# Group A of a hybrid trunk step: both values pieces of a step in one run, the recurrence in front of the fourth transposes

## The chip, the cores and the metric

The kernel runs on one core of one Trainium2 chip. The metric is the device time of the program in microseconds (us), from the start of its execution to its end. Three runs of the kernel before took 3770.87, 3778.68 and 3775.09 us: the median is 3775.09 us.

## The reference

The program is one layer of a trunk with a token mixer and a feed-forward network, for 256 context tokens and 2048 latent tokens of width 1024, all in float32. The token mixer has three groups of heads:

```python
# A: 6 query heads, 2 key/value heads of width 64, latent queries over 2048 latent + 256 context keys
sc = einsum('bqhgd,bkhd->bhgqk', q_blk, k) * scale
p = softmax(sc, axis=-1)
o = einsum('bhgqk,bkhd->bqhgd', p, v)
# B: 4 heads, two directions, chunks of 64 tokens; the recurrence over the chunks:
v_new = u_i - w_i @ s
o_i = (q_i * exp(g_i)) @ s + a_i @ v_new
s = s * exp(g_last) + einsum('bhcd,bhce->bhde', k_i * exp(g_last - g_i), v_new)
# C: 6 heads, neighbourhood attention with a bias, plus the context keys
```

Context queries of group A see the 256 context keys only. The outputs of the groups are joined, projected, normalised and go through the feed-forward network. The change touches the order of the work while group A runs; what is computed stays the same.

## The kernel before, in words

The program runs in stages: projection (`phase_b`, to about 500 us of the profile), preparation, group A (`group_a`, about 820 to 1643 us), group C (`group_c`, to about 1975 us), output projection, feed-forward network. Group B's recurrence (`recur`) has no stage of its own: it is a Python generator, and whoever runs group A or C takes one piece of it at a time with `next(rec, None)`.

**Group A.** There are 18 query tiles of 128 tokens, two to a group: groups 0 to 7 are latent tiles, group 8 the two context tiles. A group has three head pairs (`pr`), a head pair two heads (`h2`), a head two query tiles (`qi`): 12 steps per group. A step of a latent group does the following.

- It makes the scores of one head and one query tile against 2304 keys in three PSUM tiles `Sa` (1024), `Sb` (1024) and `Sc` (256); behind each, VectorE takes the row maxima (L1229) and TensorE runs one piece of the list `trs`.
- VectorE joins the three maxima (L1233), and ScalarE makes the exponentials of the three tiles into `P` (L1237). In the loop over these, pieces of other work are put in by hand, behind the first exponential (`i == 0`) and behind the second (`i == 1`).
- At its end, five transposing pieces of this step's `P` are appended to `trs`; they run during the next step.

A step of the context group has a single score tile (`n = 1`), a single exponential, and so only `i == 0`.

The lists of pieces are these. `trs`: a piece transposes four (the last: two) 128x128 blocks of `P` on TensorE into a PSUM tile `pt`, and ScalarE copies it to `PT` (L1043). `pvs`: the products with the values of the head pair before; eight pieces that each take two or three key blocks (`po`, 8 or 12 matmul instructions), and a ninth, `fin`, that transposes the result (`oT`) and scales it. `late` holds a `fin` that is due: one per head pair, so it comes in the first step of the next head pair but one. `extra` holds, in the first two head pairs of a group, an empty piece and two pieces that transpose the next group's queries (`q_stack`, `qd`). `one(q)` runs the next piece of a list, if there is one; `one(late or extra)` takes from `late` first. By these rules steps 0, 2, 3, 4, 6, 7 and 8 of a group have a late or extra piece that does work.

**The recurrence.** Its first three pieces load and prepare; then three pieces follow for each of 36 chunk pairs `n`: `w @ s` and its subtraction (L972, L983; POOL makes `Se`, L980), `v_new` (L989, L994), and outputs with the new state (L1001 to L1014, then DMAs, L1016). For even `n` the first kind has a merge for the next tile in it (`merge_u`, 32 instructions, L924, L927), and so has the second (`merge_t`, L939, L943). Each piece needs the VectorE work of the piece before. A piece starts by taking a PSUM tile `rx` with `self.rpt()`. The recurrence begins at step `RA = 6` of group A, counted over all groups (`12 * g + 4 * pr + 2 * h2 + qi`), so its loop starts at step 9 and repeats every six steps. What is left of it goes on in group C, one piece per unit from unit 6, where a unit is one head and one query tile.

**What sets the order.** TensorE's instructions are kept in program order (`self.pe` is an `InOrder`, switched on in L2108), so the place of a piece in the source is its place in TensorE's queue. The other engines' orders, DMA issues among them, come from a scheduler that goes by program order, by readiness and by priority (`tc.high_priority` moves the maxima ahead). PSUM tiles come from pools: `Sa`, `Sb` and `Sc` have one buffer each, `po` one, and the pool `A_t` (L1108) has two buffers of 2 KB under the one tag `pt`. All of `trs`, `fin`, `q_stack` and the recurrence (L1110, named `rx`) take their tile from these two; a buffer is free again when all its readers are done.

Nearly all TensorE instructions are recorded under line 37 (the `InOrder` helper), so they are told apart by tile names.

Of the kernel before, what the change touches and what calls it, by code (L numbers as in the profile page):

```python
# [59 lines left out]
class K:  # L60
# [1014 lines left out]
    def q_stack(self, t, h0, h1, pst):  # L1075

        if h0 == 0:
            self.Q[t] = [self.qp[t // 2 % 2].tile([128, 6, 128], F32R, tag=f"q{n}", name="q", bufs=2) for n in "hl"]
        self.q_split(self.Q[t][0][:, h0:h1], self.Q[t][1][:, h0:h1], self.qds[t][:, h0:h1], h1 - h0, pst)

    def q_load(self, t, pool, bufs):
        qd = self.qds[t] = pool.tile([128, 6, 2, 64], F32, tag="qd", name="qd", bufs=bufs)
        for r in range(2):
            self.sp.dma_start(qd[:, :, r, :], self.qa_d[:, t, :].rearrange("p (h d) -> p h d", d=64))
# [13 lines left out]
    def group_a(self):  # L1098
# [3 lines left out]
        with ExitStack() as es:  # L1102
# [7 lines left out]
            rec = self.rec = self.recur(self.rwk, lambda: pst.tile([128, 512], F32, tag="pt", name="rx"))  # L1110
# [46 lines left out]
            def turn(P, PTh, nk, qi):  # L1157

                def piece(k0):
                    m = min(4, nk - k0)  # L1160
                    p = pst.tile([128, 512], F32, tag="pt", name="pt")
                    for j in range(m):
                        self.pe.transpose(p[:, 128 * j:128 * j + 128],
                                          P[:, 128 * (k0 + j):128 * (k0 + j) + 128], self.ident)
                    self.evac(0, PTh[:, k0:k0 + m, 128 * qi:128 * qi + 128],
                              p[:, :128 * m].rearrange("p (j t) -> p j t", j=m))
                return [lambda k0=k0: piece(k0) for k0 in range(0, nk, 4)]

            trs, pvs, late, extra = [], [], [], []

            def one(q):
                if q:
                    q.pop(0)()

            def drain():
                for q in (trs, late, pvs, extra):
                    while q:
                        one(q)

            for g in range(len(groups)):  # L1180
                lat = g < 8
                nk = NT if lat else 2
                ks = KS if lat else KSp
                parts = [(0, 1024, "a"), (1024, 2048, "b"), (2048, 2304, "c")] if lat else [(0, 256, "")]
                n = len(parts)
                if not lat:
                    drain()
                    kc = tp.tile([128, NT, 256], F32, tag="PT", name="kc").rearrange("p a b -> p (a b)")
                    for h in range(2):
                        kv = kc[:, 2048 * h:2048 * h + 1024].rearrange("p (t r d) -> p t r d", t=8, r=2)  # L1190
                        for r in range(2):
                            nc.sync.dma_start(kv[:, :, r, :], self.c_d[1][:, h, 0:8, :])
                        for q in range(2):
                            extra.append(lambda kv=kv, h=h, q=q: self.k_split(
                                KS, kv[:, 4 * q:4 * q + 4], [(h, 4 * q + i) for i in range(4)], pst))
                    kx = kc[:, 4096:4608].rearrange("p (h t r d) -> p h t r d", h=2, t=2, r=2)
                    for h in range(2):
                        for r in range(2):
                            nc.sync.dma_start(kx[:, h, :, r, :],
                                              a["cache_c_k"][0, 0][:, h, :].rearrange("(t p) d -> p t d", p=128))  # L1200
                for pr in range(3):
                    if g + 1 < len(groups):
                        if pr < 2:
                            t = groups[g + 1][pr]
                            q_load(t)
                            extra += [lambda: None, lambda t=t: q_stack(t, 0, 4), lambda t=t: q_stack(t, 4, 6)]
                    PT = [tp.tile([128, NT, 256], F32, tag="PT", name="PT") for _ in range(2)]
                    rs = sp.tile([128, 2, 2], F32, tag="rs", name="rs", bufs=3)
                    for h2 in range(2):
                        h = 2 * pr + h2  # L1210
                        kv = h // 3
                        for qi in range(2):
                            qh, ql = (x[:, h, :] for x in Q[groups[g][qi]])
                            mx = sp.tile([128, 4], F32, tag="mx", name="mx", bufs=4)
                            sm = sp.tile([128, 4], F32, tag="sm", name="sm", bufs=4)
                            P = sp.tile([128, 2304], F32, tag="P", name="P")
                            Ss = []
                            for i, (lo_, hi_, nm) in enumerate(parts):
                                nm = nm or "abc"[(2 * h2 + qi) % 3]
                                S = psS.tile([128, 1024 if nm != "c" else 256], F32, tag="S" + nm, name="S" + nm)  # L1220
                                Ss.append(S)
                                for c0 in range(lo_, hi_, 512):
                                    c1 = min(c0 + 512, hi_)
                                    self.pe.matmul(S[:, c0 - lo_:c1 - lo_], lhsT=qh, rhs=ks[:, kv, c0:c1],
                                                   start=True, stop=False)
                                    self.pe.matmul(S[:, c0 - lo_:c1 - lo_], lhsT=ql, rhs=ks[:, kv, c0:c1],
                                                   start=False, stop=True)
                                with tc.high_priority(offset=1000):
                                    nc.vector.tensor_reduce(mx[:, i:i + 1], S[:, :hi_ - lo_], AX.X, ALU.max)  # L1229
                                one(trs)  # L1230
                            with tc.high_priority(offset=1000):
                                if n > 1:
                                    nc.vector.tensor_reduce(mx[:, 3:4], mx[:, 0:n], AX.X, ALU.max, negate=True)  # L1233
                                else:
                                    nc.vector.tensor_scalar(mx[:, 3:4], mx[:, 0:1], -1.0, None, ALU.mult)
                            for i, (lo_, hi_, nm) in enumerate(parts):
                                nc.scalar.activation(P[:, lo_:hi_], Ss[i][:, :hi_ - lo_], AF.Exp, bias=mx[:, 3:4],  # L1237
                                                     accum_out=sm[:, i:i + 1])
                                if i == 0:
                                    one(pvs)  # L1240
                                    one(trs)
                                    one(late or extra)
                                if i == 1:
                                    one(pvs)
                                    if 12 * g + 4 * pr + 2 * h2 + qi >= self.RA:
                                        next(rec, None)
                                    one(trs)
                            if n > 1:
                                nc.vector.tensor_reduce(sm[:, 3:4], sm[:, 0:n], AX.X, ALU.add)
                            nc.vector.reciprocal(rs[:, qi, h2:h2 + 1], sm[:, 3:4] if n > 1 else sm[:, 0:1])  # L1250
                            self.bg.run(2.0)
                            trs += turn(P, PT[h2], nk, qi)
                    if pvs:
                        late.append(pvs.pop())
                        while pvs:
                            one(pvs)
                    pvs += pv_pieces(g, pr, PT, rs)
# [960 lines left out]
```

## Time and profile before

| what | us |
|---|---|
| median of three runs | 3775.09 |
| the three runs | 3770.87, 3778.68, 3775.09 |
| the profiled execution | 3773.57 |
| its span, from the first to the last instruction | 3771.8 |
| group A, first score tile to last exponential | 819.5 to about 1641 |
| its last 12 steps (context group) | 1618.7 to about 1643 |
| pieces of the recurrence in group C | 1668.4 to about 1755 |

The granted TensorE clock was 0.984 on average over the span and 1.00 in group A from 900 us on. Durations in the timeline are those of instructions, which overlap on TensorE; the distance from the start of one group of matmuls to the start of the next is what a group costs.

### The profile page before, as it was taken

Reading aid. Unit: us, or ns where it says so; the run is one execution under the profiler, and the core shown is the slowest. Engines: PE = TensorE matmul, PEld = TensorE weight load, DVE = VectorE, ACT = ScalarE, POOL = GpSimd, SP = SyncE. Lnnn points to the kernel's source line nnn. Section 1 sums busy time; section 2 is a strip of 40 time slices with the busy share of each in tenths; the row PEclk is TensorE's granted clock in tenths of the full one; section 3 lists DMA queues with packets and bytes.
Section 4 is the critical chain, followed back from the end, with each engine's and each line's share of the span. In section 5 each row is a group of like instructions: output and inputs, shape, how many; then the busy total and the mean of one; then the engine's idle time right before and its main releaser. Section 6 shows DMA issues by size and latency. Waiting matters only on the chain.

```text
span 3771.8 us, 64758 instructions
## 1 busy us (share of the span) xinstructions
PE 3598.5 (95%) x24526; PEld 3154.2 (84%) x24526; DVE 2406.1 (64%) x5044; ACT 1721.0 (46%) x3541; POOL 590.1 (16%) x861
## 2 busy tenths in 40 slices
PE   8997999969999999989999989999999999999999
PEld 6886988966777777768887879999999999888887
DVE  6684477689755555558774667778778777422433
ACT  4223322236666666656775663344334334322321
POOL 0002322630000000000003411111111111000121
PEclk9998999989999999999999999999999999999999
DMA  8556877841121211155314663334334333634553
GB/s 308 183 201 182 258 224 219 206 119 47 43 53 52 53 53 52 49 142 163 99 54 164 218 189 98 102 99 126 99 98 126 102 98 93 194 116 128 199 183 128
DMA packets 647640, 501.67 MB, mean 133 GB/s; under 512 B 253521, under 2 KB 576960, under 8 KB 644768
## 3 DMA queue, kind: packets, MB, share of 16 engines
q1 hardware_dynamic: 644544, 493.93, 43.6%
q8 instruction: 193, 3.16, 0.4%
q10 hardware_dynamic: 2624, 3.55, 0.3%
q14 instruction: 119, 0.97, 0.1%
q0 software_dynamic: 160, 0.05, 0.0%
HBM read 348.66 MB, written 148.73 MB: 132 GB/s over the span
## 4 chain that ended last, share of the span: by engine, by line
PE 73%; DVE 13%; ACT 4%; DMA 4%; POOL 3%; issue 2%; SPq 1%; ACTq 0%; DVEq 0%; POOLq 0%
PE pd L37 15%; PE Y L37 10%; PE pso L37 8%; PE pt L37 7%; PE X L37 7%; PE Z L37 7%; PE po L37 6%; PE rx L37 3%; PE Sa L37 2%; DVE stmp L852 2%; PE S L37 2%; PE Sb L37 2%; DVE mx L1229 2%; PE m L37 2%; DVE sW L853 1%
## 5 line engine op out<-in xcount | busy, mean ns | idle before, releaser
L1043 ACT ACTIVATE PT<-pt 128x512 f32<-128x512 f32 (+1 forms) x600 | 332.3, 554 | 256.8 <-PE pt L37 250.0
L37 PE MATMUL Y<-hop,raw 128*128 128x384 f32 x1788 | 337.3, 337 | 5.0 <-DVE u L1929 2.9
L37 PEld LDWEIGHTS Y<-hop,raw 128*128 128x128 f32 x1788 | 313.9, 187 | 6.7 <-DVE u L1929 3.8
L37 PE MATMUL po<-PT,V 128*64 128x256 f32 (+1 forms) x3072 | 314.7, 342 | 2.2 <-ACT PT L1043 1.9
L37 PE MATMUL pso<-whi,hi 128*128 128x384 f32 (+2 forms) x864 | 288.5, 334 | 26.0 <-ACT whi L261 14.0
L37 PE MATMUL pt<-ident,P 128*128 128x128 f32 x1752 | 285.0, 280 | 15.1 <-ACT PT L1043 7.9
L37 PE MATMUL pso<-whi,lo 128*128 128x384 f32 (+2 forms) x864 | 282.4, 327 | 7.7 <-DMA lo<-hl 7.7
L37 PE MATMUL pso<-wlo,hi 128*128 128x384 f32 (+2 forms) x864 | 282.6, 327 | 0.8 <-DVE wlo L262 0.5
L37 PEld LDWEIGHTS pt<-ident,P 128*128 128x128 f32 x1752 | 200.3, 141 | 94.6 <-ACT PT L1043 35.9
L37 PEld LDWEIGHTS po<-PT,V 128*64 128x64 f32 x3072 | 181.3, 137 | 79.3 <-issue 33.8
L37 PE MATMUL X<-hop,raw 128*128 128x384 f32 x1176 | 223.4, 338 | 4.1 <-DVE raw L1766 2.3
L37 PE MATMUL Z<-hop,raw 128*128 128x384 f32 x1188 | 223.6, 336 | 0.0
L1766 DVE TENSOR_TENSOR raw<-S,raw 128x512 fp32r<-128x512 f32 x198 | 145.2, 734 | 110.7 <-ACT raw L1765 105.7
L37 PEld LDWEIGHTS X<-hop,raw 128*128 128x128 f32 x1176 | 208.0, 188 | 5.1 <-DVE raw L1766 3.1
L37 PEld LDWEIGHTS Z<-hop,raw 128*128 128x128 f32 x1188 | 208.7, 187 | 0.1
L1765 ACT ACTIVATE raw<-S 128x512 fp32r<-128x512 f32 x198 | 124.3, 629 | 172.0 <-PE X L37 66.1
L1947 POOL TENSOR_TENSOR o<-sg,p 128x384 f32<-128x384 f32 x66 | 89.2, 1352 | 711.6 <-DVE p L1946 350.8
L37 PEld LDWEIGHTS pso<-whi,hi 128*128 128x128 f32 x864 | 168.1, 195 | 30.5 <-ACT whi L261 15.6
L37 PE MATMUL pd<-wd,ao 128*128 128x512 f32 x756 | 185.5, 394 | 0.0
L37 PE MATMUL pd<-wd,hop 128*128 128x512 f32 x756 | 183.0, 392 | 0.0
L980 POOL TENSOR_TENSOR rSe<-rS,eh 64x128 f32<-64x128 f32 x144 | 54.9, 400 | 811.8 <-DVE rS L1012 780.9
L37 PEld LDWEIGHTS pso<-whi,lo 128*128 128x128 f32 x864 | 167.6, 194 | 10.9 <-DMA lo<-hl 9.1
(360 smaller groups left out, 8283.9 us busy)
## 6 DMA issues: line engine op xcount, KB each, us to landing
hr<-a SPq DMA_DIRECT2D x72, 704.0 KB, 4.5
wr<-in_w_gu_dram SPq DMA_DIRECT2D x66, 512.0 KB, 4.0
wr<-in_w_gu_dram SPq DMA_DIRECT2D x132, 256.0 KB, 3.1
a<-o SPq DMA_DIRECT2D x396, 64.0 KB, 1.6
wm<-in_w_mod_dram SPq DMA_DIRECT2D x48, 512.0 KB, 4.4
hi<-hh SPq DMA_DIRECT2D x36, 512.0 KB, 5.0
lo<-hl SPq DMA_DIRECT2D x36, 512.0 KB, 6.1
st<-ptk SPq DMA_DIRECT2D x18, 768.0 KB, 3.9
```

Of the source, the lines that this page charges most:

```text
L37: r = f(*x, **kw)
L852: v.tensor_tensor(tv, M[:n, c0:c1, c0:i], M[:n, c0:i, i].unsqueeze(1).to_broadcast([n, m, k]), ALU.mult)
L853: v.tensor_reduce(M[:n, c0:c1, i], tv, AX.X, ALU.add)
L980: nc.gpsimd.tensor_tensor(Se[hh[x], d], S[hh[x], d, :, hh[x]], e.unsqueeze(2).to_broadcast([64, 2, 64]), ALU.mult)
L1043: self.nc.scalar.activation(out, p, AF.Copy)
L1229: nc.vector.tensor_reduce(mx[:, i:i + 1], S[:, :hi_ - lo_], AX.X, ALU.max)
L1765: self.nc.scalar.activation(hi, raw, AF.Copy)
L1766: self.nc.vector.tensor_tensor(lo, raw, hi.bitcast(F32), ALU.subtract)
L1947: nc.gpsimd.tensor_tensor(o[:, 0], sg, p1, ALU.mult)
```

## The change

Two places in the loop over the exponentials change. Behind the first exponential the values piece is taken out, and the recurrence's piece (with its condition) takes its place in front of the fourth transposing piece. Behind the second exponential two values pieces follow one another, and then comes the fifth transposing piece.

```diff
                                 if i == 0:
-                                    one(pvs)
+                                    if 12 * g + 4 * pr + 2 * h2 + qi >= self.RA:
+                                        next(rec, None)
                                     one(trs)
                                     one(late or extra)
                                 if i == 1:
                                     one(pvs)
-                                    if 12 * g + 4 * pr + 2 * h2 + qi >= self.RA:
-                                        next(rec, None)
+                                    one(pvs)
                                     one(trs)
```

A latent step still runs two values pieces, two transposing pieces, one late or extra piece and one piece of the recurrence in this loop. In the context group, where only `i == 0` is reached, a step used to run a values piece and no piece of the recurrence; now it runs a piece of the recurrence and no values piece, and the values pieces run in the loop at the end of the head pair (L1253 to L1256), which is not changed.

## The prediction

> **What bounds the kernel now.** I read the page first, for the span and the engine that fills it.
>
> ```profile
> span 3771.8 us, 64758 instructions
> PE 3598.5 (95%) x24526; PEld 3154.2 (84%) x24526; DVE 2406.1 (64%) x5044; ACT 1721.0 (46%) x3541; POOL 590.1 (16%) x861
> ```
>
> The profiled run took 3773.57 us, 1.8 us more than its span; the median of the three timed runs is 3775.09, so the sum below is made against 3773.6 and 1.5 us are within the spread. A busy share over the whole program says little about one stage, so next came the table by stage: one stretch of group A's even part, and the whole of its last 12 short steps (the context query tiles). Columns: stretch, length, busy time of PE, weight loads, DVE, ACT, POOL, granted clock, DMA.
>
> ```profile
> 1100.00:1200.00 100.00, 98.70 (x968) 75.29 (x964) 55.83 (x121) 68.67 (x143) 6.05 (x16) 1.00 0.19 50
> 1618.70:1643.00 24.30, 17.35 (x104) 10.88 (x103) 13.39 (x50) 14.42 (x45) 0.39 (x3) 1.00 0.06 18
> ```
>
> In the even part TensorE is busy 98.7 of 100 us and the others far less: a microsecond in which TensorE stands still is a microsecond of the end, and no other engine is close. In the last 12 steps TensorE has 24.3 - 17.35 = 7 us free. TensorE issues in program order, so the order of the pieces is the subject. Part of the timeline of one even step with a piece of the recurrence and one "late" piece (here `oT`) follows; columns: start, length, engine, line, what.
>
> ```profile
> 1212.47 0.60 PE L37 MATMUL pt<-ident,P 128*128 128x128 f32 x4
> 1212.82 1.17 PE L37 MATMUL Sb<-KA,q 128*128 128x512 f32 x4
> ...
> 1214.46 1.28 ACT L1043 ACTIVATE PT<-pt 128x512 f32<-128x512 f32 x2 [0.76 <-PE pt L37]
> 1214.51 0.60 PE L37 MATMUL pt<-ident,P 128*128 128x128 f32 x4
> 1215.04 1.08 PE L37 MATMUL po<-PT,V 128*64 128x256 f32 x8
> ...
> 1215.87 1.12 ACT L1237 ACTIVATE P<-Sa,mx 128x1024 f32<-128x1024 f32 x1
> 1216.05 0.66 PE L37 MATMUL pt<-ident,P 128*128 128x128 f32 x4
> 1216.54 0.38 PE L37 MATMUL pt<-ident,oT 128*128 128x128 f32 x2
> 1216.86 1.08 PE L37 MATMUL po<-PT,V 128*64 128x256 f32 x8
> ...
> 1217.45 1.12 ACT L1237 ACTIVATE P<-Sb,mx 128x1024 f32<-128x1024 f32 x1
> 1217.78 0.66 PE L37 MATMUL rx<-rS,rsT 128*64 128x128 f32 x8
> ...
> 1218.36 0.44 PE L37 MATMUL pt<-ident,P 128*128 128x128 f32 x2
> 1218.47 0.87 DVE L983 TENSOR_TENSOR rv<-rst,rx 64x256 f32<-64x256 f32 x2 [1.02 <-PE rx L37]
> ```
>
> Matmuls overlap, so I price by the distance of starts. The order is: third transposing piece (1214.51), a values piece (`po`), fourth transposing piece (1216.05), late piece (1216.54), values, recurrence (`rx`), fifth transposing piece (1218.36). Transposes, late pieces and recurrence all take their PSUM from one pool of two buffers (`pt`, the same pool as `rx`). That is the resource the change touches: whoever holds a buffer long must have other work behind him.
>
> **The change, part by part.** In a step with three score tiles the recurrence piece goes from between the second values piece and the fifth transposes to between the third and the fourth transposes; both values pieces come together after the late piece. No instruction is added or removed.
>
> (a) The late piece behind the recurrence. New order of buffer takers: third transposes, recurrence, fourth transposes, late, fifth. With two buffers the late piece needs the one that the recurrence holds (or the one of the fourth transposes, which ScalarE empties no sooner, behind an exponential). Before, the recurrence piece was followed by transposes 5, a score tile and transposes 1 before its buffer mattered; now only the fourth transposes lie between. Call E the start of TensorE's next work after the recurrence piece. Without a wait the late piece would start at E + 0.49 (1216.54 - 1216.05: the length of four transposes). With it, it starts when VectorE has read the buffer. The recurrence has three kinds of piece, and two of them also carry, every other round, the merge for the next tile:
>
> ```profile
> 1194.15 0.44 PE L37 MATMUL pt<-ident,P 128*128 128x128 f32 x2
> 1194.25 0.29 DVE L927 TENSOR_TENSOR rU<-rx,nb 128x128 f32<-128x128 f32 x1 [3.73 <-PE rx L37]
> 1194.46 0.86 DVE L983 TENSOR_TENSOR rv<-rst,rx 64x256 f32<-64x256 f32 x2
> ```
>
> ```profile
> 1202.11 0.44 PE L37 MATMUL pt<-ident,P 128*128 128x128 f32 x2
> 1202.22 1.19 DVE L943 COPY rsy<-rx 32x128 f32<-32x128 f32 x4 [3.56 <-PE rx L37]
> 1203.42 0.42 DVE L994 COPY rv<-rx 64x256 f32<-64x256 f32 x1
> ...
> 1205.33 0.60 ACT L1043 ACTIVATE PT<-pt 128x512 f32<-128x512 f32 x1 [0.78 <-PE pt L37]
> 1205.98 0.66 PE L37 MATMUL pt<-ident,P 128*128 128x128 f32 x4 [0.45 <-ACT PT L1043]
> ...
> 1209.51 0.66 PE L37 MATMUL rx<-rS,rsT 128*64 128x128 f32 x8
> 1211.26 0.44 PE L37 MATMUL pt<-ident,P 128*128 128x128 f32 x2
> 1211.43 0.87 DVE L1012 TENSOR_TENSOR rS<-rSe,rx 64x256 f32<-64x256 f32 x2 [0.34 <-PE rx L37]
> ...
> 1212.33 0.42 DVE L1014 COPY ro<-rx 128x256 f32<-128x256 f32 x1
> ```
>
> A released buffer is used 0.05 us later (the transfer of 1205.33 ends at 1205.93, the transposes start at 1205.98, after a wait that shows what a held buffer does). So the buffer is free at: first kind without merge, 0.11 + 0.87 + 0.05 = E + 1.03 (E is 1218.36); with merge, 1195.32 - 1194.15 + 0.05 = E + 1.22; second kind without merge, 0.11 + 2 x 0.42 + 0.05 = E + 1.00; with merge, 0.11 + 1.19 + 2 x 0.42 + 0.05 = E + 2.19; third kind, 1212.75 - 1211.26 + 0.05 = E + 1.54. Less 0.49, TensorE waits 0.54, 0.73, 0.51, 1.70 and 1.05 us. VectorE is then free (it has finished the step's maxima and the next tile of scores comes later), so nothing queues ahead of these reads.
>
> How often: a late piece with work comes, by the code, in 7 of 12 steps (one `oT` per head pair; four query pieces in the first eight steps). The recurrence loop starts in step 9, has period 6, so the pairing is fixed: steps 0 and 6 of a group meet the first kind plain (0.54 each), 2 and 8 the third (1.05 each), 3 the first with merge (0.73), 4 the second with merge (1.70), 7 the second plain (0.51). Sum: 1.08 + 2.10 + 0.73 + 1.70 + 0.51 = 6.1 us per group of 12. Steps 9 to 95 are 87, 7.25 groups: **+44 us**. Behind the waiting late piece stand on TensorE both values pieces, the fifth transposes and the next scores; ScalarE and VectorE then wait for those scores, so nothing catches up.
>
> (b) The recurrence behind the third transposes needs the buffer of the second. That is free at 1214.46 + 0.60 + 0.05 = 1215.11 in the step above, and TensorE could be there at 1214.51 + 0.53 = 1215.04: 0.07 us x 87 = **+6 us**. The fourth transposes have the recurrence piece (0.6 us and more) as cover for the third ones' transfer.
>
> (c) Waits that go. TensorE's idle time in front of the transposes and of two kinds of recurrence piece, over all of group A's even part:
>
> ```profile
> L37 PE MATMUL pt<-ident,P 128*128 128x128 f32 x1728 | 279.9, 280 | 10.4 <-ACT PT L1043 7.6 <-DVE q L1037 2.2 <-DVE ro L1014 0.2
> L37 PE MATMUL rx<-rS,rsT 128*64 128x128 f32 x464 | 38.2, 280 | 3.6 <-ACT PT L1043 3.6
> L37 PE MATMUL rx<-rv,rsy 128*64 128x64 f32 x464 | 26.8, 225 | 2.1 <-ACT PT L1043 2.1
> ```
>
> Together 10.4 + 3.6 + 2.1 = 16 us. The recurrence no longer follows the late piece, and its buffer is free before the next step's transposes; a little of the 16 belongs to the start-up. I take **-14 us** (bounds -6 and -16).
>
> (d) The change of shape between 128*128 and 128*64 work costs: four transposes take 1212.82 - 1212.47 = 0.35 in front of scores, 0.53 in front of values; values in front of transposes take 1.01 (1216.05 - 1215.04), in front of the 128*64 recurrence 0.92. That is 0.18 + 0.09 = 0.27 for going and coming back. The old step goes to 128*64 twice (values; values with recurrence), the new one twice (recurrence; values with values). So: **0**. [...]
>
> (e) The last 12 steps. They have a single score tile, and the second place (`i == 1`) is never reached: the old code advances no recurrence there and does one values piece a step; the new one advances 12 pieces and leaves the values to the end of each head pair. These 12 pieces are missing later in group C, which has one per unit. Group C with them and without (values matmuls, 28 per two units), and the recurrence alone:
>
> ```profile
> 1703.80:1755.20 51.40, 10.50 (x168) 9.07 (x168) 1.64 (x6) 1.00 0.58 162
> 1800.00:1860.00 60.00, 19.24 (x308) 16.59 (x308) 3.06 (x11) 1.00 0.23 53
> ```
>
> ```profile
> 1703.80:1755.20 51.40, 15.77 (x320) 13.86 (x320) 13.05 (x34) 1.00 0.58 162
> ```
>
> Six pairs of units take 51.4, 8.57 each; eleven pairs take 60, 5.45 each. So 12 pieces cost group C 6 x 3.12 = 18.7 us, which go. In the last 12 steps they bring 15.8 us of TensorE; with all 7 us of holes filled that is +8.8. With every VectorE reading (13.05) waited for in full it is 15.8 + 13.05 = +28.8, their DMAs included since each round's loads have less time than in long steps. The middle, +18.8, is my value: a chain in which each piece needs the one before, beside about 1.4 us of own work per step. Net **0**, bounds -10 and +10.
>
> SP's and POOL's queues get the same DMAs and products a few us earlier; POOL is busy 6 of 100 us, so nothing in (a) to (d) hangs on them.
>
> Sum: 3773.6 + 44 + 6 - 14 + 0 + 0 = 3809.6, **3810 us**, about 1% slower.
>
> **The rivals.** *Faster, 0.14:* the late piece does not wait, because the pool hands it a buffer that is free; then (c) and the better half of (e) remain: 3773.6 - 14 - 10 = 3750. Against it: the three readers above start after E and none lasts under 0.84 us, while only 0.49 us of work covers them. *No change, 0.12:* the wait is there but at half its size, because the late piece gets whichever of the two buffers is free first and the third kind's copy is not waited for: 22 + 6 - 14 - 10 = +4, 3778. [...] *Much slower, 0.06:* the late piece is handed the buffer of the fourth transposes, and ScalarE's queue has their transfer behind both exponentials. In the step above these start at 1215.87 and last 1.12 each, so the transfer (0.60) ends near 1218.7. The recurrence starts at 1215.1, so the late piece could go at 1215.1 + 0.58 + 0.49 = 1216.2 behind the shortest piece (1218.36 - 1217.78) and at 1217.3 behind the longest (1211.26 - 1209.51 = 1.75): waits of 2.5 to 1.4 us, some 2 for each of 7, 14 per group of 12: 3773.6 + 101 + 6 - 14 = 3867. It decides from the point at which the transfer stands behind the second exponential; in the step above that one starts at 1217.45, late enough to leave room in front. *My forecast, 0.64,* own range 3785 to 3835 (waits a quarter smaller or larger: 11 us; bounds of (c) and (e)).
>
> **How the numbers follow.** What a measurement of this kernel can tell is about 0.2%, 7.5 us. Slower by more: the forecast and the last two rivals, 0.74; within: 0.12; faster: 0.14. The range leaves out most of the faster case and the worst one: 3766 to 3842. The likeliest is 3810.
>
> **What would show it.** TensorE's idle time in front of the late pieces is the third figure here:
>
> ```profile
> L37 PE MATMUL pt<-ident,qd 128*128 128x128 f32 x96 | 15.8, 274 | 0.5 <-DVE q L1037 0.4
> L37 PE MATMUL pt<-ident,oT 128*128 128x128 f32 x46 | 8.9, 275 | 0.2 <-ACT PT L1043 0.2
> ```
>
> In the profile after, the 0.5 + 0.2 us rise to some 40 us, ended by VectorE's recurrence lines (L983, L994, L943, L1012, L1014 moved by the edit); the idle time in front of `rx` falls to a few us or moves to the 0.07 of (b); an even group of 12 steps gets 36 / 7.25 = 5 us longer; the last 12 steps last about 43 us instead of 24.3 and group C ends its recurrence 12 units earlier. I am wrong if the idle time in front of the late pieces stays under 10 us, or if group A's even part gets shorter.

## The result and the profile after

| what | before | after |
|---|---|---|
| median, us | 3773.88 (4 runs, 3770.87 to 3778.68) | 3827.27 (4 runs, 3823.57 to 3834.43) |
| profiled execution, us | 3773.57 | 3827.81 |
| its span, us | 3771.8 | 3826.0 |

The ratio is 1.0141, 95% interval [1.0129, 1.0153]: the changed kernel is slower, 17 us more than the forecast of 3810. I split the 54.2 us that the span grew by the first matmuls of the stages, in us:

| stretch | before | after | difference |
|---|---|---|---|
| up to the first score tile of group A | 819.5 | 821.7 | +2.2 |
| groups 0 and 1 | 194.9 | 206.4 | +11.5 |
| groups 2 to 7 | 604.3 | 633.4 | +29.1 |
| the 12 context steps | 25.0 | 50.0 | +25.0 |
| group C | 332.2 | 319.5 | -12.7 |
| behind it | 1795.9 | 1795.0 | -0.9 |

An even group of 12 steps took 98.54 us before and takes 103.50 after: +4.96, where 5.0 was forecast. The first and the last two rows of the table are not from the latent steps; the first is the scatter of a stretch that the edit doesn't touch.

First the page of the kernel after, span and busy times. TensorE works only some 16 us more than before (3598.5), so the growth is mostly waiting:

```profile
span 3826.0 us, 64816 instructions
PE 3614.6 (94%) x24526; PEld 3164.4 (83%) x24526; DVE 2415.7 (63%) x5044; ACT 1726.8 (45%) x3541; POOL 589.0 (15%) x861
```

The table by stage shows it for 100 us of even groups and for the whole of the context steps (columns as in the prediction). In the first, TensorE was busy 98.7 us and is now busy 95.4. The second stretch has doubled, and TensorE stands still in it for 50.00 - 37.15 = 12.9 us; its granted clock is 0.90, not 1.00.

```profile
1200.00:1300.00 100.00, 95.41 (x932) 72.47 (x929) 55.70 (x117) 65.01 (x133) 6.04 (x16) 1.00 0.18 49
```

```profile
1661.50:1711.50 50.00, 37.15 (x488) 28.98 (x486) 28.17 (x88) 15.34 (x47) 7.25 (x21) 0.90 0.29 80
```

Now the groups of instructions of TensorE from 810 to 1700 us: count, then busy time and mean, then idle time in front and what ended it.

```profile
L37 PE MATMUL pt<-ident,P 128*128 128x128 f32 x1748 | 283.1, 280 | 5.5 <-ACT PT L1043 2.5 <-DVE ro L1014 2.4 <-DVE rv L994 0.2
...
L37 PE MATMUL rx<-rS,rsT 128*64 128x128 f32 x520 | 43.6, 287 | 3.3 <-ACT PT L1043 0.9 <-DVE rS L1012 0.8 <-DVE KA L1032 0.4
L37 PE MATMUL rx<-rv,rsy 128*64 128x64 f32 x528 | 32.7, 231 | 2.8 <-ACT PT L1043 1.6 <-DVE rs L1250 0.9
L37 PE MATMUL pt<-ident,qd 128*128 128x128 f32 x96 | 17.0, 286 | 22.8 <-PE pt L37 9.0 <-DVE rv L983 5.4 <-DVE rv L994 3.2
L37 PE MATMUL pt<-ident,oT 128*128 128x128 f32 x50 | 10.5, 293 | 20.8 <-ACT PT L1043 7.1 <-DVE ro L1014 7.0 <-DVE rv L983 3.6
```

The last two rows are the late pieces: 0.7 us of idle time have become 43.6, ended by the recurrence's reads (`rv`, `ro`) and, in part, by ScalarE's transfers. A releaser "PE pt" is only the work in front, so for those 9.0 us the view doesn't name the holder. The transposes' idle time is down to 5.5 (point (c) below).

Three steps in the timeline of the kernel after; the weight loads (PEld) are left out. Step 0 of a group, the recurrence's first kind without merge:

```profile
1238.72 0.66 PE L37 MATMUL rx<-rS,rsT 128*64 128x128 f32 x8
1238.77 0.41 DVE L1229 TENSOR_REDUCE mx<-Sc 128x1 f32<-128x256 f32 x1
1239.39 0.66 PE L37 MATMUL pt<-ident,P 128*128 128x128 f32 x4
1239.44 0.42 DVE L983 TENSOR_TENSOR rv<-rst,rx 64x256 f32<-64x256 f32 x1 [0.25 <-PE rx L37]
1239.89 0.16 DVE L1233 TENSOR_REDUCE mx<-mx 128x1 f32<-128x3 f32 x1
1240.08 0.41 DVE L983 TENSOR_TENSOR rv<-rst,rx 64x256 f32<-64x256 f32 x1
1240.14 1.11 ACT L1237 ACTIVATE P<-Sa,mx 128x1024 f32<-128x1024 f32 x1 [0.81 <-DVE mx L1233]
1240.64 0.41 PE L37 MATMUL pt<-ident,oT 128*128 128x128 f32 x2 [0.60 <-DVE rv L983]
```

The late piece starts 1.25 us behind the fourth transposes, where it needs 0.49: a wait of 0.76. The second subtraction ends at 1240.08 + 0.41 = 1240.49, and 0.15 later the late piece starts, where the prediction took 0.05 for a release. Between the two reads stands the joining of the step's maxima (L1233), which the prediction held to be finished by then.

Step 3, the first kind with the merge. Both buffers come free here at almost the same time: VectorE's second read ends at 1266.75, ScalarE's transfer of the fourth transposes at 1266.87. The late piece starts 0.15 behind the read, the same distance as in step 0, and the view puts its wait down to that read: it has the recurrence's buffer.

```profile
1265.89 0.86 DVE L983 TENSOR_TENSOR rv<-rst,rx 64x256 f32<-64x256 f32 x2
...
1266.27 0.60 ACT L1043 ACTIVATE PT<-pt 128x512 f32<-128x512 f32 x1
...
1266.90 0.41 PE L37 MATMUL pt<-ident,qd 128*128 128x128 f32 x2 [0.66 <-DVE rv L983]
```

Step 4, the second kind with the merge:

```profile
1275.13 0.66 PE L37 MATMUL pt<-ident,P 128*128 128x128 f32 x4
...
1275.23 1.19 DVE L943 COPY rsy<-rx 32x128 f32<-32x128 f32 x4 [1.17 <-PE rx L37]
1275.82 0.60 ACT L1043 ACTIVATE PT<-pt 128x512 f32<-128x512 f32 x1 [0.46 <-PE pt L37]
1276.31 1.11 ACT L1237 ACTIVATE P<-Sb,mx 128x1024 f32<-128x1024 f32 x1
1276.43 0.86 DVE L994 COPY rv<-rx 64x256 f32<-64x256 f32 x2
1276.47 0.44 PE L37 MATMUL pt<-ident,oT 128*128 128x128 f32 x2 [0.69 <-ACT PT L1043]
```

Here the late piece runs at 1276.47, while the recurrence's tile is still being read until 1277.29. It was given the other buffer, that of the fourth transposes, whose transfer ScalarE ran ahead of the second exponential, to 1275.82 + 0.60 = 1276.42.

### The profile page after: what moved, and what is told of

Read it like the earlier page. It is cut to its first block, busy times and chain, and to the rows that moved or that the text cites. A ratio compares the mean times of both kernels' runs of the same rounds, so it can differ in the third digit from the quotient of the medians.

```text
span 3826.0 us, 64816 instructions
## 1 busy us (share of the span) xinstructions
PE 3614.6 (94%) x24526; PEld 3164.4 (83%) x24526; DVE 2415.7 (63%) x5044; ACT 1726.8 (45%) x3541; POOL 589.0 (15%) x861
## 5 line engine op out<-in xcount | busy, mean ns | idle before, releaser
L37 PE MATMUL po<-PT,V 128*64 128x256 f32 (+1 forms) x3072 | 296.0, 340 | 2.7 <-ACT PT L1043 2.4
L37 PEld LDWEIGHTS po<-PT,V 128*64 128x64 f32 x3072 | 189.9, 138 | 78.9 <-issue 20.1
L1229 DVE TENSOR_REDUCE mx<-Sa 128x1 f32<-128x1024 f32 (+1 forms) x102 | 120.0, 1177 | 112.6 <-PE Sa L37 112.6
```

What stands on the lines that cost most here:

```text
L37: r = f(*x, **kw)
```

## The experiments

All times are medians, each with its ratio to the kernel before as it ran on the same chip in the same session. The kernel before took 3771.49, 3774.36 and 3776.97 us in the three sessions, so runs of different sessions are compared by their ratios. Group lengths are from the start of one group's first `Sa` to the next one's.

**The context steps apart: `ctx_without`, `ctx_only`, `ctx_half`.** In `ctx_without` the edit holds in the latent steps alone (context steps then run neither a values nor a recurrence piece there); in `ctx_only` in the context steps alone; `ctx_half` is the kernel before with the recurrence in every second context step.

```diff
 ctx_without (against after)
-if 12 * g + 4 * pr + 2 * h2 + qi >= self.RA:
+if 12 * g + 4 * pr + 2 * h2 + qi >= self.RA and lat:
 ctx_only (against before, at i == 0)
-one(pvs)
+if lat: one(pvs)
+else: next(rec, None)
 ctx_half: the same, with "elif qi == 0:" for "else:"
```

> The changed kernel, but the recurrence is not advanced in the 12 context steps (condition `and lat` added); group C runs those 12 pieces again. Theory (the late piece waits for the recurrence's buffer in the even steps; the context steps are a cost of their own): the even part stays 41 us longer, the last 12 steps fall from 50 back to 25 us and group C goes from 320 back to 332 us: 3827 - 25 + 13 = 3815 us. Rival (all of the loss is in the even part, the context steps are free because group C gains as much): 3827 us, no change.

> The kernel before, with the context steps alone as in the change (a piece of the recurrence instead of a values piece), the latent steps untouched. Theory: +12 us, 3786 us, and no wait in front of the late pieces. Rival (moving the pieces out of group C pays for them): 3774 us.

> The kernel before, with a piece of the recurrence in every second context step instead of a values piece (6 pieces; ctx_only had 12). If each piece costs there what it costs in ctx_only (26 us for 12 in the context steps, 17 us for 12 back in group C): half of +9.5, 3772 + 5 = 3777 us. If the holes of the context steps (7 us) take the first pieces and only the chain of 12 in a row is dear (each needs VectorE's work on the one before): 6 x 1.3 - 6 = +2 there and -8.4 in group C, 3766 us.

`ctx_without` took 3815.52 us, ratio 1.0116 [1.0101, 1.0131], with even groups of 103.46; `ctx_only` 3781.28, 1.0024 [1.0014, 1.0034], with 98.5: its context steps last 51.3 us (+26.3) and its group C 315.4 (-16.8). `ctx_half` took 3775.99, 1.0006 [0.9996, 1.0015]: context steps 33.6 (+8.6), group C 324.1 (-8.1). So the edit has two separate costs: the latent steps are most of it (1.2%), and the 12 context steps a quarter of a per cent. For six pieces, one in every second step, the trade of holes against group C is even; going on to twelve costs twice as much as the first six did (+17.7 against +8.6) and saves as much (8.7 against 8.1).

**Who holds the buffer: `late_behind`, `rec_first`, `read_twice`.** `late_behind` moves nothing but the late piece, behind the two values pieces, in latent steps, measured against `ctx_without`; like that one it runs no piece of the recurrence in the context steps. `rec_first` keeps the recurrence's early place but puts a values piece behind it. `read_twice` is the kernel after with one more VectorE read of each recurrence tile.

```diff
 late_behind (against ctx_without)
-one(late or extra)                        # at i == 0, latent steps
+one(pvs); one(pvs); one(late or extra)    # at i == 1, then one(trs)
 rec_first (against before)
+next(rec, None)                           # at i == 0, ahead of one(pvs), latent steps
-next(rec, None)                           # at i == 1
 read_twice (against after, at the end of each recurrence piece)
+v.tensor_copy(jk, x[:, 0:256])
```

> The changed kernel with the context steps as in ctx_without, and in latent steps the late piece moved behind the run of values: recurrence, fourth transposes; values, values, late, fifth transposes. The same instructions and the same two changes to 128x64 work per step. Theory (the wait is for a buffer that has only 0.5 us of cover): the 43.6 us of idle time in front of qd and oT fall under 5, waits of the old order do not come back: about 3774 + 7 - 14 + 5 = 3772 us, a group of 12 steps at 97 to 98.5 us. Rival (the loss comes from the order of transposes, recurrence and values itself, their changes of shape): stays near 3815 us.

> The other half alone: in latent steps the recurrence moves in front of the transposes behind the first exponential, but the values stay where they were, so: recurrence, values, fourth transposes, late; values, fifth transposes. The context steps run no piece of the recurrence and keep their values piece. Theory of the two buffers: 1.0 or 1.45 us of values plus 0.5 us of transposes now cover the recurrence's buffer, which is enough for all kinds but the one with the merge of the second kind (0.7 us, once per group); old waits go: 3772 - 14 + 7 + 5 = 3769 us, a group at 97.5 to 98 us, idle time in front of qd and oT under 10 us. Rival (the early place of the recurrence costs by itself): like ctx_without, 3815 us.

> The changed kernel, and in group A each piece of the recurrence ends with one more VectorE copy of its PSUM buffer (128x256, 0.42 us) into a tile that nobody reads: the buffer is held 0.42 us or more longer, TensorE's instructions are the same. Theory (the late piece waits until VectorE has read the recurrence's buffer): 0.42 us more in 7 of 12 steps, 51 steps, +22 us, idle time in front of qd and oT from 43.6 to about 65 us; with 12 x 0.42 = 5 us in the context steps 3827 + 27 = 3854 us. Rival (the late piece waits for ScalarE's transfer of the fourth transposes, or for the changes of shape): no change in the even part, 3827 to 3832 us.

`late_behind` took 3773.93, ratio 1.0007 [0.9997, 1.0016]; even groups 97.76. With cover between the recurrence and the late piece the whole 1.2% is gone, though the recurrence stays ahead of the fourth transposes and the values stay together. Its late pieces in the groups of instructions (same stretch), where what is left is the wait for the queries' load at the start of group C:

```profile
L37 PE MATMUL pt<-ident,qd 128*128 128x128 f32 x114 | 21.3, 294 | 6.0 <-DMA qd<-cq 4.9 <-DVE oa L1147 0.7 <-DMA rlo<-low 0.2
L37 PE MATMUL pt<-ident,oT 128*128 128x128 f32 x59 | 13.4, 302 | 2.8 <-ACT PT L1043 1.0 <-ACT oT L1136 1.0 <-DVE sW L853 0.4
```

`rec_first` took 3779.45, 1.0016 [1.0007, 1.0025]; even groups 99.1, not the 97.5 to 98 that I expected. One values piece covers most readers, but not the long ones: waits of 0.81 in step 4, 0.29 in step 8 and 0.25 in step 2 remain.

`read_twice` took 3843.09, 1.0186 [1.0172, 1.0200]: slower than after, as a held buffer must be and a matter of places alone would not be. But the even group grew by 1.7 us (103.50 to 105.20), not by 2.9. The waits grew by about 0.33 in steps 0, 2, 6, 7 and 8 and by nothing in steps 3 and 4 (1.32 to 1.34 and 1.34 to 1.34 from fourth transposes to late piece): the two steps with a merge. There its late piece starts 0.05 behind ScalarE's transfer, while the added copy still reads the recurrence's tile, so it has the other buffer; in the kernel after only step 4 is seen to have it. Its late pieces' rows have the added copy (`rjk`) as a releaser, with 51.9 us of idle time where 65 were expected:

```profile
L37 PE MATMUL pt<-ident,qd 128*128 128x128 f32 x96 | 17.2, 289 | 27.5 <-ACT PT L1051 8.7 <-issue 7.7 <-DVE rjk L883 5.5
L37 PE MATMUL pt<-ident,oT 128*128 128x128 f32 x50 | 10.6, 293 | 24.4 <-DVE rjk L883 14.8 <-ACT PT L1051 9.1 <-ACT oT L1145 0.5
```

**The price of changing shape: `run_only`, `one_run`.** Both leave one stretch of 128*64 work per step where before and after have two. `run_only` moves the first values piece to the second and leaves the recurrence behind them; `one_run` puts the recurrence, both values pieces, the fourth transposes, the late piece and the fifth transposes in this order.

```diff
 run_only (against before)
-one(pvs)                                  # at i == 0
+one(pvs)                                  # at i == 1, ahead of the recurrence
 one_run (latent steps)
+next(rec, None)                           # at i == 0, alone
+one(pvs); one(pvs); one(trs); one(late or extra); one(trs)   # at i == 1
```

> The other half alone: the two values pieces in one run behind the second exponential, the recurrence behind them where it was before; so third transposes, fourth transposes, late; values, values, recurrence, fifth transposes. TensorE goes to 128x64 work once per step, not twice. By the price of the pair (0.27 us x 96 steps) alone: -26 us, 3748 us. Theory of the two buffers: the fourth transposes now wait for the second ones' transfer (0.25 us, 96 steps, +24) and the late piece for the third ones' (0.2 us, 56 steps, +11), old waits go (-14): 3774 - 26 + 24 + 11 - 14 = 3769 us.

> All 128x64 work of a latent step in one run: recurrence behind the first exponential; behind the second values, values, then fourth transposes, late, fifth transposes. Context steps without the recurrence. By the price of a pair of changes of shape, 0.27 us in 96 steps: -26 us. Theory of the two buffers: the recurrence's buffer has the run of values (2 us) as cover, but the fifth transposes follow the fourth closely and wait for their transfer, 0.45 us in 56 steps, +25; old waits go (-14), the recurrence's 0.07 us stays (+7): 3772 - 26 + 25 - 14 + 7 = 3764 us. If the price of a pair is all there is: 3739 us.

`run_only` took 3781.46, 1.0030 [1.0019, 1.0041] (even groups 99.2), `one_run` 3786.81, 1.0034 [1.0021, 1.0047] (99.25). Both of my expectations fell: one pair of changes less per step, 26 us by the prediction's 0.27 in 96 steps, gains nothing here. For `one_run` the profile shows what stands against the expected gain. In front of its transposes, 810 to 1700 us, stands this idle time, 25.7 us more than the 15.1 that the kernel before has in the same stretch:

```profile
L37 PE MATMUL pt<-ident,P 128*128 128x128 f32 x1752 | 275.9, 279 | 40.8 <-ACT PT L1043 30.1 <-ACT P L1237 4.8 <-DVE oa L1147 4.0
```

Step 0 of a group of it shows how: fourth transposes, late piece and fifth transposes come within 1.6 us, and the two buffers must be emptied in between.

```profile
1220.69 0.66 PE L37 MATMUL pt<-ident,P 128*128 128x128 f32 x4
...
1221.18 0.38 PE L37 MATMUL pt<-ident,oT 128*128 128x128 f32 x2
1221.60 0.49 DVE L1147 TENSOR_TENSOR oa<-pt,rs 128x128 f32<-128x128 f32 x2 [1.46 <-PE pt L37]
...
1222.23 0.41 PE L37 MATMUL pt<-ident,P 128*128 128x128 f32 x2 [0.67 <-DVE oa L1147]
```

In `run_only` the same row reads 25.8, that is 10.7 more; the rest of its missing gain is not located.

**A version without either cost: `late_behind_ctx`.** It is `late_behind` with the context steps as they were.

```diff
 (against late_behind, at i == 0)
+if not lat: one(pvs)
```

> As late_behind in the latent steps (recurrence in front of the fourth transposes, both values pieces, then the late piece, then the fifth transposes), and the context steps as before, with their values piece in its old place. late_behind took 3773.93 beside 3771.49 for before, with even groups of 97.75 us instead of 98.5 and a first group longer by as much. Theory (the only harm of the order is the held buffer in front of the late piece, and here fourth transposes and two values pieces cover it): even groups 97.7 to 97.8, 6 x 0.75 = 4.5 us less than before in them, the context steps back at 25 us, and 0.9995 of before or a little less, 3768 to 3774 if before takes 3774; no late wait over 0.1. Rival (the place costs as much as it saves, whatever the cover): even groups at 98.5 and a time 5 us or more above before.

It took 3778.26 beside 3776.97 for the kernel before: ratio 1.0000 [0.9991, 1.0009]. The theory's group length came (97.80), the gain did not: groups 2 to 7 took 5.1 us less than before (599.2 against 604.3), but groups 0 and 1 together 2.6 more and the context steps 1.7 more (26.7 against 25.0; over 1615 to 1645 us the granted clock was 0.89, in the kernel before 1.00). No order that was tried is shown to be faster than the one before.

## Why the prediction was right, and where its terms were off

**The bound, and (a) as a mechanism: right, and shown.** The late piece behind the recurrence waits for a buffer of the pool. Cover in its place removes the whole cost (`late_behind`), longer reading adds to it (`read_twice`). The waits per kind of step, from the distance of starts less 0.49:

| step of the group | predicted | measured |
|---|---|---|
| 0 and 6, first kind plain | 0.54 | 0.76, 0.72 |
| 3, first with merge | 0.73 | 0.83 |
| 7, second plain | 0.51 | 0.62 |
| 4, second with merge | 1.70 | 0.85 |
| 2 and 8, third kind | 1.05 | 1.11, 1.16 |
| sum of a group | 6.1 | 6.05 |

The reads themselves were sized well; that the sum is right to 0.1 is luck, since errors cancel. Six steps wait 0.06 to 0.22 longer than forecast, 0.8 in all. In each of them the late piece starts 0.10 to 0.15 behind VectorE's last read, where the prediction took 0.05 from a release by ScalarE. And the step "so nothing queues ahead of these reads" failed in steps 0 and 6, where the join of the maxima slips between the two reads, 0.2 us. Against this, "ScalarE empties no sooner, behind an exponential" failed in step 4, which waits 0.85 less: the transfer came between the two exponentials, and the late piece had that buffer. There the rival *Much slower* was right about which buffer and *No change* about a wait of half the size, in one step of seven; what decides for *Much slower*, the transfer behind the second exponential, was not reached.

**(a) in groups 0 and 1: mis-sized.** The forecast had the loop there for 15 of its 87 steps, about 15 / 12 x 5.0 = 6 us; it was +11.5. Two things are in it. Group 1 is 7.8 us longer, where an even group is 5.0: VectorE works on the triangular solves (`sW`) there, and the prediction's free VectorE does not exist. First step of group 1, kernel after:

```profile
921.34 0.66 PE L37 MATMUL rx<-rS,rsT 128*64 128x128 f32 x8
...
921.61 1.20 DVE L1229 TENSOR_REDUCE mx<-Sb 128x1 f32<-128x1024 f32 x1
922.74 0.40 DVE L1229 TENSOR_REDUCE mx<-Sc 128x1 f32<-128x256 f32 x1
...
923.79 0.42 DVE L983 TENSOR_TENSOR rv<-rst,rx 64x256 f32<-64x256 f32 x1
924.24 0.15 DVE L853 TENSOR_REDUCE sW<-stmp 64x2 f32<-64x4 f32 x1
924.32 0.38 DVE L852 TENSOR_TENSOR stmp<-sW 64x88 f32<-64x88 f32 x2
924.73 0.41 DVE L983 TENSOR_TENSOR rv<-rst,rx 64x256 f32<-64x256 f32 x1
...
925.29 0.41 PE L37 MATMUL pt<-ident,oT 128*128 128x128 f32 x2 [2.70 <-DVE sW L853]
```

The subtractions start 1.8 us after the recurrence's matmuls (921.34 + 0.66). VectorE is late: it ends the step's maxima at 923.14, 1.1 us behind those matmuls, where in step 0 above it ended them 0.2 ahead. Then solves stand in front of the first subtraction and between the two. The late piece waits 2.70. The idle time in front of the late pieces from 821 to 1028 us is 7.2 + 6.4 us in the kernel after:

```profile
L37 PE MATMUL pt<-ident,qd 128*128 128x128 f32 x24 | 4.5, 299 | 7.2 <-ACT PT L1043 3.1 <-issue 2.0 <-DVE rv L983 1.4
...
L37 PE MATMUL pt<-ident,oT 128*128 128x128 f32 x8 | 1.7, 294 | 6.4 <-DVE sW L853 2.7 <-ACT PT L1043 2.7 <-DVE ro L1014 1.0
```

The other thing is group 0, 3.7 us longer. Its steps 9 to 11, where the loop starts, have no late piece with work and did not grow (24.8 us against 25.3); steps 6 and 8 grew by 3.0 and 1.0. They come ahead of the loop, and the forecast counted nothing in them. `run_only`, which leaves the recurrence where it was, has the same step 6 (11.23 us against 11.22), so that growth is not the recurrence's buffer. Together these two groups were longer in every other order of the latent steps that was tried (by 1.5 us in `late_behind` to 14.4 in `ctx_without`, which has the latent steps of the kernel after); how the solves' own arrangement shifts with the order was not isolated.

**(b) and (c): right within what can be read.** From the third transposes to the recurrence it takes 0.61 instead of 0.53 us, near the predicted 0.07 more. For (c) these are the rows of the kernel before over the longer stretch of 810 to 1700 us:

```profile
L37 PE MATMUL pt<-ident,P 128*128 128x128 f32 x1752 | 285.0, 280 | 15.1 <-ACT PT L1043 7.9 <-ACT P L1237 4.5 <-DVE q L1037 2.2
...
L37 PE MATMUL rx<-rS,rsT 128*64 128x128 f32 x504 | 41.5, 280 | 3.7 <-ACT PT L1043 3.6
L37 PE MATMUL rx<-rv,rsy 128*64 128x64 f32 x512 | 29.7, 226 | 2.1 <-ACT PT L1043 2.1
```

They add up to 20.9, and those of the kernel after to 5.5 + 3.3 + 2.8 = 11.6 (what is (b) stands among them only as far as the modelled ends show it). So 9.3 us went, inside the bounds of 6 and 16. What an even group leaves for (c), 4.96 - 6.05 - 12 x 0.08 = -2.05, comes to 15 us in 7.25 groups, near the 14 forecast.

**(d): right for this edit, not as a currency.** The change keeps the number of changes, and no such saving appeared. Where the number really falls by one per step (`one_run`), the 26 us expected from it stand against 25.7 us more idle time in front of the transposes, which then follow one another too closely. The chance of 0.74 for a slower kernel counts 0.04 for one pair of changes less per step (0.27 x 87 = 23 us); no run here shows such a pair as time gained.

**(e): the term that failed, with the solves.** The "Net 0, bounds -10 and +10" was +25.0 - 12.7 = +12.3 here, beyond the upper bound, and +26.3 - 16.8 = +9.5 in `ctx_only`, just within it. Its two halves:

Group C saved less than the 18.7. The six pairs of units that took 51.40 us with the recurrence take this without it (values matmuls, columns: length, PE, weight loads, ACT, clock, DMA):

```profile
1770.04:1808.28 38.24, 10.50 (x168) 9.05 (x168) 1.62 (x6) 1.00 0.35 86
```

That is 6.37 a pair, where the prediction took 5.45 from a later stretch: 13.2 us saved, not 18.7. The step that failed is the price of a pair without the recurrence from other pairs than the ones that it goes from; by the starts of the values matmuls two of the pairs there last 7.48 and 8.60 us with no recurrence in them.

The context steps cost more than +18.8. The recurrence's chain stands in them, as forecast, and the clock falls. Two 5 us stretches of the context steps after:

```profile
1675.00:1680.00 5.00, 4.53 (x54) 3.63 (x54) 1.96 (x6) 1.05 (x4) 0.00 (x0) 0.50 0.21 58
1680.00:1685.00 5.00, 4.48 (x45) 3.53 (x44) 2.69 (x10) 0.95 (x3) 0.04 (x1) 0.59 0.02 3
```

```profile
1668.01 1.44 PE L37 MATMUL rx<-rv,rst 128*64 128x64 f32 x32
```

```profile
1681.74 2.62 PE L37 MATMUL rx<-rv,rst 128*64 128x64 f32 x32
```

Rows of the timeline: the 32 matmuls of the third kind last 1.44 at full clock and 2.62 inside that stretch. As an estimate, if all busy time goes with the clock as those 32 matmuls did (1.44 / 2.62 = 0.55), the 9.0 us of work in the two stretches would have been 4.53 x 0.50 + 4.48 x 0.59 = 4.9 at full clock, so the fall costs at most 4.1 of the 6.2 us by which +25.0 exceeds +18.8. `ctx_half`, whose context steps keep a clock of 1.00, comes out at +8.6 for six pieces, near half of 18.8; but its pieces also stand further apart, so it does not separate the clock from the chain. That the fall makes the difference is argued from this, not shown, since no run could hold the clock.

Against the forecast of +36 the profiled run grew by 54.2: 4.6 more in the latent steps (5.3 more in groups 0 and 1, 0.7 less in the others), 12.3 from (e), 1.3 from stretches that the edit doesn't touch. The sign and the mechanism stood; two mis-sized terms make up the 17 us.

## What to carry to other kernels

When a piece is moved in a queue with few PSUM buffers, write down the new order of the buffer's takers and, for every taker, the work that now lies between the release it needs and itself; the late piece had 0.5 us of cover where the buffer came 1.1 to 1.65 us later, and two values pieces behind the same place made the cost vanish with the same two buffers. Work put together to save changes of shape also pushes the rest together, and the buffers between those pieces can then take back as much as was expected of it (in `one_run` 25.7 us of idle time, where a saving of 26 was expected). A price for work "without X" is read from the very stretch that X leaves, and an engine counted as free is checked in each stage, the first groups too.

## What the runs showed of the hardware that was not expected

In the context steps with the recurrence, where TensorE stands still for a quarter of the time (12.9 of 50.0 us), the granted clock fell for 10 us (0.50 over 1675 to 1680, 0.59 over 1680 to 1685) and came back to 1.00 (1685 to 1690). The kernel before has such a fall at the start of group C:

```profile
1655.00:1660.00 5.00, 2.22 (x24) 1.80 (x20) 2.20 (x12) 3.30 (x10) 0.00 (x0) 1.00 1.00 279
1660.00:1665.00 5.00, 3.36 (x16) 3.39 (x17) 1.77 (x6) 0.53 (x2) 0.00 (x0) 0.53 0.95 193
1665.00:1670.00 5.00, 5.00 (x49) 4.50 (x48) 3.27 (x10) 3.02 (x8) 0.00 (x0) 0.78 0.58 158
```

The kernel after has falls there too (0.83 over 1710 to 1720, 0.50 over 1730 to 1735), so the one in its context steps is an added one. The fall in the kernel before comes with a stop of 4.43 us:

```profile
1661.64 0.66 PE L37 MATMUL pt<-ident,qd 128*128 128x128 f32 x2 [4.43 <-DMA qd<-cq]
```

The fall in the context steps after has no such stop ahead of it: in the 20 us up to 1675 TensorE's longest is this one of 1.09 us.

```profile
1671.36 0.41 PE L37 MATMUL pt<-ident,P 128*128 128x128 f32 x2 [1.09 <-DVE ro L1014]
```

Nor does such a fall need the recurrence: `late_behind_ctx`, whose context steps run the pieces of the kernel before, had a clock of 0.89 over 1615 to 1645 us and took 1.7 us longer in them. What sets these falls stays open, and so does, with one profile of each kernel, whether the order of work brings one or each execution falls in its own places. In the context steps after it was worth at most some 4 us by the estimate under (e).
